# Two-part products with 512 moving columns for the memory keys, MoBA and cross-attention queries

## Chip, cores and metric

The program runs on one core of a Trainium2 chip (trn2). The metric is device time of one execution in microseconds (us), the median of several runs. The engines are TensorE (PE; its weight loads are shown apart as PEld), VectorE (DVE), ScalarE (ACT), GpSimd (POOL) and SyncE (SP), each with a queue that it works off in order.

## What is computed

A decoder trunk of two layers on 256 tokens of width 1024. Each layer is a SwiGLU half-step, a mixing step (RWKV-7 on 8 heads beside causal attention, called MoBA, on 8 heads), cross-attention to 256 memory tokens, and a second SwiGLU half-step:

```python
x = x + 0.5 * swiglu_ffn(rms_norm(x, ffn1_norm_g[l]), ffn1_w_in[l], ffn1_w_out[l])
proj = rms_norm(x, mix_norm_g[l]) @ w_mix_in[l]        # RWKV columns, then q_m, k_m, v_m of MoBA
x = x + concat([rwkv7_time_mix(...), moba_attention(q_m, k_m, v_m, rel_bias)]) @ w_mix_out[l]
x = x + memory_cross_attention(rms_norm(x, ..), rms_norm(mem, ..), w_q[l], w_kv[l], w_o[l])
x = x + 0.5 * swiglu_ffn(rms_norm(x, ffn2_norm_g[l]), ffn2_w_in[l], ffn2_w_out[l])
```

All is float32. The products that concern us are `q_m` and `k_m` (512 columns each), the memory keys (1024 columns of `w_kv`) and the cross-attention queries `h @ w_q` (1024 columns).

## The kernel before

**Two parts.** An operand of a large product is split into a high part that TensorE takes exactly (`fp32r`) and the low rest: `split` (L85) makes the high part with a copy on ACT and the rest with a subtraction on DVE. A product is the sum of high times high, high times low and low times high. `mm3` (L96) issues these as three matmuls into one sum.

**Weights.** `load` (L101) brings a unit of 1 MB into one of two `raw` buffers with a transfer on SP; `unit` splits it into two halves `whi`, `wlo` (five buffers each; two ACT copies, two DVE subtractions of 1024 columns). A half is one column tile: 128 output columns of all 1024 rows, which are 8 K-tiles. A `raw` buffer is free for the next transfer once its second DVE subtraction is done.

**Feature-major products.** The operand is `xt`, laid out `[k // 2][:, k % 2, high or low, token]`, so that high and low tokens of one K-tile lie side by side (512 columns). `col_a` (L250) makes one column tile, `[128, 256]`, with 8 times `mm3`: 24 matmuls of 256 moving columns. `proj_a` (L256) puts the two column tiles of a unit side by side in one PSUM bank. The `ffn` (L308) already uses another form (L329 to L338): high weights times both parts in one matmul of 512 columns, low weights times the high part in one of 256, then an ACT copy of the second half of the bank to `z` and a DVE addition of the first half to it.

**The mixing step** (`mix`, L849). `rwkv` (L531) is written as a generator; between its steps TensorE is given other work: `early` (MoBA queries and keys, four units), then, after the operand of the memory tokens is made (`mem_operand`, L368: eight ACT copies, eight DVE operations of 256 columns), `others`: MoBA's heads, `late` (memory keys, four units), values of the memory tokens, and the first output products. `early` and `late` both call `pieces` (L880): two column tiles by `col_a` into one bank, then one ACT copy of 512 columns to `dst`. The generators yield a number of microseconds that steers how much filling is put between two steps. In RWKV's stretch of masked chunk products each chunk and half takes four matmuls on PE and two DVE products (`XB`, `ZL`, L653 and L655); an inverse by rows follows on DVE (`pr`, `mb`, L691).

**Cross-attention** (`xattn`, L378). `scores(h)` makes a head's queries with `proj_a`, splits them from PSUM (one ACT copy, one DVE subtraction of 512 columns, `put_pair`), multiplies them with the keys, and takes the softmax; `mixv(h - 1)` follows with the values of the head before.

**Buffers and order.** Four PSUM banks carry the tag `acc`; `z` has tag `k1` with six buffers, which RWKV's `ub`, `mb`, `pr`, `T1`, `TB`, `R` share. The order on each queue is made by the framework's planner from priorities, dependencies and its own costs; it may place instructions of different lines between each other.

Of the kernel before, what the change touches and what calls it, by code (L numbers as in the profile page):

```python
# [12 lines left out]
OP = mybir.AluOpType  # L13
# [3 lines left out]
S = 256  # L17
L = 2
DFF = 2816
NB = DFF // 256  # L20
KT = D // 128
# [26 lines left out]
def body(tc, ctx, I, out):  # L48
# [52 lines left out]
    def load(src, cuts, heap=False):  # L101
        """A unit of weights: its two halves' exact high and low parts, and the pieces that make them."""
        raw = wp.tile([128, 2048], FT, name=nm("raw"), tag="raw", bufs=2)
        loads.append(nc.sync.dma_start(raw, src).ins)
        halves, pieces = [], []
        for i in range(2):
            if heap:
                hi, lo = (H([128, 1024], FR, "wb") for _ in range(2))
            else:
                hi, lo = (wp.tile([128, 1024], FR, name=nm(t), tag=t, bufs=WB) for t in ("whi", "wlo"))  # L110
            w = 1024 // cuts
            for c in range(0, 1024, w):
                pieces.append((hi[:, c:c + w], lo[:, c:c + w], raw[:, i * 1024 + c:i * 1024 + c + w]))
            halves.append((hi, lo))
        return halves, pieces
# [11 lines left out]
    def rsqrt(v, n, tag):  # L127
        """1 / (RS sqrt(v)): the exponent's half as a first guess, a third-order step and a Newton
        step, each step's factor left in."""
        r = SM([128, n], name="rs", tag=tag)  # L130
        t = SM([128, n], name="rt", tag=tag)
        V.tensor_scalar(r.bitcast(I32), v.bitcast(I32), -0.5, float(0x5F3759DF), op0=OP.mult, op1=OP.add)

        def square():
            if n == 1:
                stt(t, r, v, r, OP.mult, OP.mult)
            else:
                tt(t, r, r, OP.mult)
                tt(t, t, v, OP.mult)

        square()
        stt(t, t, -10.0 / 3.0, t, OP.add, OP.mult)
        stt(r, t, 5.0, r, OP.add, OP.mult)
        square()
        stt(r, t, -3.0 * (8.0 / 3.0) ** 2, r, OP.add, OP.mult)
        return r

# [43 lines left out]
    def XT(tag="xn"):  # L191
        """Operand with 1024 rows on partitions: [k // 2][:, k % 2, high or low, token]."""
        return [H([128, 2, 2, S], FR, "xt", tag) for _ in range(4)]
# [10 lines left out]
    def normed(g):  # L204
        """Norm of x with gain g into a new operand, a tile of 128 tokens at a time."""
        xT = []

        def do(t, pieces=()):
            """Between its feature tiles, pieces of weights are split."""
# [21 lines left out]
    def proj_b(xT, ws):  # L231
        """Token-major [2][128, 512]; all of the first 128 tokens, then the others."""
        ws = [tuple(a.rearrange("p (k n) -> p k n", k=2) for a in h) for h in ws]
        acc = []
        for t in range(2):
            acc.append(BANK("acc"))
            for k in range(KT):
                mm3(acc[t], tok(xT, k, t), tuple(a[:, k % 2, :] for a in ws[k // 2]),
                    k == 0, k == KT - 1)
            yield acc[t]  # L240
# [3 lines left out]
    def ahead(src, u):  # L244
        """A unit of the next stage's first block, split ahead."""
        if u == 0:
            ready.clear()
        ready.extend(unit(src[u], CU["b"], True))

    def col_a(acc, xT, w):  # L250
        """Feature-major [128, 256] of one column tile."""
# [3 lines left out]

    def proj_a(xT, src, cuts):  # L256
        """Feature-major [128, 2, 256] of one unit of two column tiles."""
# [5 lines left out]
    def proj_out(lhs, src, nk, scale, post, following=None, split_tail=False):  # L263
        """x += scale * lhs @ w, token-major over 1024 columns; units of two K-tiles. post(t)
        follows each tile of tokens. following: the weights of the next stage's first block."""
# [42 lines left out]
    def ffn(xT, w_in, w_out, post, following, early=()):  # L308
# [17 lines left out]
        for j in range(2, DFF // 128):  # L326
            sums = []
            for half_ in unit(w_in[j], CU["ffn"]):
                w = tuple(a.rearrange("p (k m) -> p k m", k=KT) for a in half_)  # L329
                acc = BANK("acc")  # L330
                for k in range(KT):
                    mm(acc, w[0][:, k, :], xT[k // 2][:, k % 2].rearrange("p i t -> p (i t)"),
                       k == 0, False)
                    mm(acc[:, 0:S], w[1][:, k, :], feat(xT, k)[0], False, k == KT - 1)
                z = SM([128, S], name="z", tag="k1")
                copy(z, acc[:, S:2 * S])
                tt(z, acc[:, 0:S], z, OP.add)
                sums.append(z)  # L338
# [39 lines left out]
    def xattn(l, xT, kTf, vx, post, following):  # L378
        """vx: the values of the memory tokens by pairs of heads, and what makes the second pair."""
# [8 lines left out]
        def scores(h):  # L388
            put_pair(qT, h, proj_a(xT, I["w_q"][l, h], CU["q"]))
# [63 lines left out]
    def moba(qT, kT, v, yT):  # L453
        """Steps of one head each: its scores, then the values of the head before."""
# [76 lines left out]
    def rwkv(l, xT, yT):  # L531
        """Yields the time, in us of TensorE, that its next step waits for."""
# [10 lines left out]
        def shifted(u, dst):  # L543
            """One unit of two column tiles: p + (shift(p) - p) * mu, tokens along the free axis."""
# [33 lines left out]
        # decay products inside a chunk  # L578
# [9 lines left out]
        # normalised keys, negated  # L588
# [16 lines left out]
        # k * (1 + (a - 1) * k_a)  # L605
# [17 lines left out]
        # operands of the chunk products  # L623
# [17 lines left out]
        # products inside a chunk: transposed, masked  # L641
# [26 lines left out]
        # inverse of I - U: 16x16 diagonal blocks, one to a partition  # L668
# [8 lines left out]
        # token-major b/G, k/G  # L677
# [87 lines left out]
        # bonus and gate: y * (g * ln_g) + (r k r_k v + ln_b) * g  # L765
# [7 lines left out]
        # chunks in order  # L773
        for c in range(NCH):
# [48 lines left out]
            # group norm over each head, two chunks at once  # L823
# [25 lines left out]
    def mix(l, xT, post):  # L849
# [8 lines left out]
        def v_block(mT, n):  # L858
            """Values of the memory tokens, heads 2n and 2n + 1: [token tile][128, high or low, 512]."""
# [20 lines left out]
        def pieces(xT, src, dst):  # L880
            """Two column tiles into dst [128, 2, 256], one at a time."""
            acc = BANK("acc").rearrange("p (c t) -> p c t", c=2)
            for c, w in enumerate(unit(src, CU["qk"])):
                col_a(acc[:, c, :], xT, w)
                if c:
                    copy(dst, acc)
# [102 lines left out]
def _onehot(np):  # L989
    """Column m: the bucket of distance 255 - m."""  # L990
# [7 lines left out]
def _layout(np, z):  # L998
    z = {k: np.asarray(v) for k, v in z.items()}

    def k_rows(w, kt, n):
        """(L, K, N) into units of kt K-tiles: (L, K/(128 kt), 128, kt*N)."""
# [4 lines left out]
    def col_pairs(w):  # L1007
        """(L, 1024, N) into units of two column tiles: (L, N/256, 128, 2*8*128)."""
# [4 lines left out]
    def blocks(w):  # L1013
        """(L, 1024, N) into blocks of 512 columns, two units each: (L, N/256, 128, 4*512)."""
# [4 lines left out]
    def gate_up(w):  # L1019
        """The first 256 gate and 256 up columns as a block, then a gate and an up column tile a unit."""  # L1020
# [62 lines left out]
```

## Time and profile before

| | us |
|---|---|
| median of 3 runs | 1321.84 (1321.48 to 1321.96) |
| span of the profiled execution, first to last instruction | 1317.5 |
| PE busy in it | 1294.7 |
| DVE busy | 913.3 |
| ACT busy | 769.3 |
| HBM read | 217.70 MB, 168 GB/s over the span |

The runs' times hold some 4.3 us that lie outside the span; another time of the profiled execution is not given. Busy times of engines overlap. The granted TensorE clock was 0.998 of its full speed over the span. Matmuls overlap in the records (a matmul of 256 columns is shown with 0.28 us and the next one begins 0.12 us after it), so the pace of TensorE is read from starts, not from durations.

### The profile page before, as it was taken

What the parts mean: (1) busy time and instruction counts of PE and PEld (TensorE: products, weight loads), DVE (VectorE), ACT (ScalarE), POOL (GpSimd) and SP (SyncE); (2) the same over time, 40 slices, a digit from 0 to 9 for tenths busy, and PEclk for the clock granted to TensorE, in tenths of its full rate; (3) what the DMA queues carried; (4) which work ended last, traced back from release to release, by engine and by line L of the source; (5) the groups of instructions that cost most, each with busy time, mean ns of one, the idle gap of its engine ahead of it and who ended that gap; (6) DMA issues with size and microseconds to landing.
All of it is one profiled execution on the core that took longest, in us unless ns stands there. A gap on an engine that the chain in (4) does not pass through costs nothing.

```text
span 1317.5 us, 21984 instructions
## 1 busy us (share of the span) xinstructions
PE 1294.7 (98%) x8722; PEld 1109.7 (84%) x8722; DVE 913.3 (69%) x1699; ACT 769.3 (58%) x1465; POOL 33.7 (3%) x49
## 2 busy tenths in 40 slices
PE   7999999999999999999999999999999999999997
PEld 5888888998878988888888888889887798888886
DVE  6766656698588676665577775558976976776644
ACT  6755546749656555555455554475685565655533
POOL 0000000020000000000000000000200000000000
PEclk9999999999999999999999999999999999999999
DMA  6775563334234445555735556433341354355552
GB/s 213 263 278 193 192 255 113 130 127 140 87 134 166 149 151 174 187 193 192 250 105 191 190 192 223 177 128 128 129 146 66 128 193 157 147 187 189 185 179 92
DMA packets 32919, 221.22 MB, mean 168 GB/s; under 512 B 4248, under 2 KB 4384, under 8 KB 7344
## 3 DMA queue, kind: packets, MB, share of 16 engines
q1 hardware_dynamic: 30064, 210.54, 45.0%
q0 software_dynamic: 2176, 8.44, 1.9%
q8 instruction: 68, 1.11, 0.3%
q10 hardware_dynamic: 576, 0.85, 0.2%
q14 instruction: 35, 0.29, 0.1%
HBM read 217.70 MB, written 3.68 MB: 168 GB/s over the span
## 4 chain that ended last, share of the span: by engine, by line
PE 85%; DVE 8%; ACT 4%; DMA 2%; issue 1%; ACTq 0%
PE acc L94 77%; PE pm L94 5%; DVE wlo L77 2%; DVE ZL L77 1%; PE tr L188 1%; DVE XB L77 1%; ACT whi L83 1%; DMA raw<-in_w_k_dram 1%; ACT xt L83 1%; ACT junk L174 0%; DVE wb L77 0%; PE acc L500 0%; DMA raw<-in_w_q_dram 0%; DVE rt L80 0%; ACT e L400 0%
## 5 line engine op out<-in xcount | busy, mean ns | idle before, releaser
L94 PE MATMUL acc<-xt,whi 128*128 128x512 f32 (+1 forms) x2496 | 681.6, 344 | 1.0 <-DVE xt L80 0.7
L77 DVE TENSOR_TENSOR wlo<-raw,whi 128x1024 fp32r<-128x1024 f32 (+1 forms) x456 | 465.1, 1034 | 257.9 <-ACT whi L83 256.5
L83 ACT ACTIVATE whi<-raw 128x1024 fp32r<-128x1024 f32 (+1 forms) x456 | 405.3, 906 | 331.8 <-PE acc L94 240.7
L94 PE MATMUL acc<-xt,wlo 128*128 128x256 f32 x1888 | 529.8, 281 | 0.2 <-DVE wlo L77 0.2
L94 PEld LDWEIGHTS acc<-xt,whi 128*128 128x128 f32 x2496 | 431.7, 189 | 64.5 <-issue 2.8
L94 PEld LDWEIGHTS acc<-xt,wlo 128*128 128x128 f32 x1888 | 357.3, 189 | 3.0 <-issue 1.4
L94 PE MATMUL acc<-whi,hT 128*128 128x512 f32 x704 | 220.9, 393 | 0.0
L94 PEld LDWEIGHTS acc<-whi,hT 128*128 128x128 f32 x704 | 132.3, 188 | 29.9
L94 PE MATMUL acc<-wlo,hT 128*128 128x512 f32 x352 | 138.2, 393 | 0.0
L94 PEld LDWEIGHTS acc<-wlo,hT 128*128 128x128 f32 x352 | 66.2, 188 | 14.7
L77 DVE TENSOR_TENSOR z<-acc,z 128x256 f32<-128x256 f32 x160 | 66.7, 417 | 0.3 <-ACT z L83 0.2
L83 ACT ACTIVATE xt<-tr,par 128x128 fp32r<-128x128 f32 x128 | 43.9, 364 | 32.9 <-PE tr L188 18.4
L94 PE MATMUL acc<-wb,xt 128*128 128x512 f32 x240 | 61.4, 399 | 0.0
L83 ACT ACTIVATE z<-acc 128x256 f32<-128x256 f32 x160 | 58.6, 366 | 1.8 <-PE acc L94 1.7
L94 PE MATMUL acc<-whi,xt 128*128 128x512 f32 x160 | 57.2, 420 | 1.2 <-ACT xt L83 1.1
L94 PEld LDWEIGHTS acc<-wb,xt 128*128 128x128 f32 x240 | 43.4, 188 | 9.4 <-ACT xt L83 0.4
L80 DVE SCALAR_TENSOR_TENSOR xt<-tr,par,xt 128x128 fp32r<-128x128 f32 x128 | 41.4, 345 | 11.2 <-ACT xt L83 11.0
L174 ACT ACTIVATE junk<-x 128x512 f32<-128x512 f32 x36 | 22.7, 632 | 33.9 <-DVE x L80 25.1
L94 PE MATMUL acc<-whi,oT 128*128 128x512 f32 x128 | 40.3, 393 | 0.0
L77 DVE TENSOR_TENSOR z<-z,z 128x256 f32<-128x256 f32 x80 | 34.0, 425 | 8.4 <-DVE z L77 0.9
L83 ACT ACTIVATE hT<-z 128x256 fp32r<-128x256 f32 x80 | 32.2, 403 | 10.3 <-DVE z L77 10.1
L94 PEld LDWEIGHTS acc<-whi,xt 128*128 128x128 f32 x160 | 31.2, 198 | 8.2 <-ACT xt L83 1.4
(224 smaller groups left out, 1226.2 us busy)
## 6 DMA issues: line engine op xcount, KB each, us to landing
raw<-in_w_f1i_dram SPq DMA_DIRECT2D x44, 1024.0 KB, 4.8
raw<-in_w_f2i_dram SPq DMA_DIRECT2D x44, 1024.0 KB, 4.7
raw<-in_w_f1o_dram SPq DMA_DIRECT2D x22, 1024.0 KB, 4.8
raw<-in_w_mixa_dram SPq DMA_DIRECT2D x22, 1024.0 KB, 4.7
raw<-in_w_f2o_dram SPq DMA_DIRECT2D x22, 1024.0 KB, 4.8
raw<-in_w_k_dram SPq DMA_DIRECT2D x8, 1024.0 KB, 4.8
raw<-in_w_v_dram SPq DMA_DIRECT2D x8, 1024.0 KB, 4.8
raw<-in_w_mixo_dram SPq DMA_DIRECT2D x8, 1024.0 KB, 4.7
```

Source lines behind the costliest of these rows:

```text
L77: V.tensor_tensor(out=out_, in0=a, in1=b, op=op)
L80: V.scalar_tensor_tensor(out_, a, s, b, op0=op0, op1=op1)
L83: return A.activation(out_, in_, AF.Copy, **k)
L94: nc.tensor.matmul(o, a, b, start=start, stop=stop, skip_group_check=True)
L174: marks["square"] = A.activation(junk, xt[:, n * 512:(n + 1) * 512], AF.Square, scale=1.0 / 32.0, accum_out=ss[:, n:n + 1]).ins
L188: nc.tensor.transpose(p[:, k, :], xs[:, k * 128:(k + 1) * 128], ident)
```

## The change

`col_sum` is a new function, taken from the body of `ffn`, which now calls it; what `ffn` issues stays the same. `pieces` and `scores` call it in place of `col_a` and `proj_a`. `proj_a` with `col_a` remain for RWKV's own columns. Comments and docstrings fall away too.

```diff
+    def col_sum(dst, xT, w):
+        w = tuple(a.rearrange("p (k m) -> p k m", k=KT) for a in w)
+        acc = BANK("acc")
+        for k in range(KT):
+            mm(acc, w[0][:, k, :], xT[k // 2][:, k % 2].rearrange("p i t -> p (i t)"), k == 0, False)
+            mm(acc[:, 0:S], w[1][:, k, :], feat(xT, k)[0], False, k == KT - 1)
+        z = SM([128, S], name="z", tag="k1")
+        copy(z, acc[:, S:2 * S])
+        if dst is None:
+            dst = z
+        tt(dst, acc[:, 0:S], z, OP.add)
+        return dst
...
         def scores(h):
-            put_pair(qT, h, proj_a(xT, I["w_q"][l, h], CU["q"]))
+            for c, w in enumerate(unit(I["w_q"][l, h], CU["q"])):
+                split(qT[h][:, c, 0, :], qT[h][:, c, 1, :], col_sum(None, xT, w))
...
         def pieces(xT, src, dst):
-            acc = BANK("acc").rearrange("p (c t) -> p c t", c=2)
             for c, w in enumerate(unit(src, CU["qk"])):
-                col_a(acc[:, c, :], xT, w)
-                if c:
-                    copy(dst, acc)
+                col_sum(dst[:, c, :], xT, w)
                 yield 2.6
```

Over both layers it touches 16 column tiles each of `early`, `late` and `scores`: 48 tiles of 8 K-tiles.

## Rows read from the trace of the kernel before

**Rows 1.** The page: the span, busy time by engine, and the chain that ended last by engine.

```profile
span 1317.5 us, 21984 instructions
PE 1294.7 (98%) x8722; PEld 1109.7 (84%) x8722; DVE 913.3 (69%) x1699; ACT 769.3 (58%) x1465; POOL 33.7 (3%) x49
PE 85%; DVE 8%; ACT 4%; DMA 2%; issue 1%; ACTq 0%
```

**Rows 2.** Busy time by stretch; columns: stretch, its length, then PE, PEld, DVE, ACT and POOL busy (instructions), granted clock, DMA share, GB/s. In order: RWKV's masked chunk products with `early`, in both layers; the rest of RWKV with `others`, in both layers; cross-attention, in both layers.

```profile
268.00:300.00 32.00, 32.00 (x266) 30.68 (x266) 30.54 (x53) 17.23 (x26) 7.89 (x8) 1.00 0.38 132
914.00:946.00 32.00, 32.00 (x266) 30.54 (x264) 29.07 (x50) 17.22 (x27) 7.89 (x8) 1.00 0.34 114
300.00:382.00 82.00, 80.90 (x1133) 65.38 (x1132) 58.87 (x143) 58.76 (x139) 3.52 (x6) 1.00 0.32 111
946.00:1028.00 82.00, 80.07 (x1130) 65.10 (x1128) 59.64 (x144) 58.27 (x137) 1.50 (x2) 1.00 0.30 105
412.00:462.00 50.00, 49.40 (x358) 45.61 (x357) 34.50 (x67) 29.52 (x64) 0.00 (x0) 1.00 0.42 148
1062.00:1108.00 46.00, 45.62 (x339) 42.34 (x338) 31.39 (x60) 26.21 (x55) 0.55 (x1) 1.00 0.44 158
```

**Rows 3.** Timeline of PE in `early`, layer 0: the low-weight matmul of a K-step and the one 26 K-steps later, without other work between them.

```profile
287.67 0.28 PE L94 MATMUL acc<-xt,wlo 128*128 128x256 f32 x1
...
297.03 0.28 PE L94 MATMUL acc<-xt,wlo 128*128 128x256 f32 x1
```

**Rows 4.** Timeline of PE in `ffn`: the low-weight matmul of a K-step and a later one; 28 K-steps apart in layer 0, 11 K-steps apart in layer 1.

```profile
59.81 0.28 PE L94 MATMUL acc<-xt,wlo 128*128 128x256 f32 x1
...
69.70 0.28 PE L94 MATMUL acc<-xt,wlo 128*128 128x256 f32 x1
...
690.91 0.27 PE L94 MATMUL acc<-xt,wlo 128*128 128x256 f32 x1
...
694.72 0.28 PE L94 MATMUL acc<-xt,wlo 128*128 128x256 f32 x1
```

**Rows 5.** Tiles named `z`: durations in ns (min/median/max); the copy and the addition of `ffn`'s form, and the two operations of a split of 256 columns.

```profile
L83 ACT ACTIVATE z<-acc x160: 362/365/385, 32.9 to 1250.1; 128x256 f32<-128x256 f32 x160
L77 DVE TENSOR_TENSOR z<-acc,z x160: 413/417/426, 34.3 to 1251.4; 128x256 f32<-128x256 f32 x160
L83 ACT ACTIVATE hT<-z x80: 397/401/420, 37.6 to 1252.4; 128x256 fp32r<-128x256 f32 x80
L77 DVE TENSOR_TENSOR hT<-z,hT x80: 349/418/427, 38.9 to 1252.8; 128x256 fp32r<-128x256 f32 x80
```

**Rows 6.** Timeline of ACT, 262 to 300 us: the copies of `early` at the ends of its first three units, and the memory operand behind a weight split.

```profile
275.49 0.60 ACT L83 ACTIVATE mqk<-acc 128x512 f32<-128x512 f32 x1 [3.70 <-PE acc L94]
...
285.44 0.60 ACT L83 ACTIVATE mqk<-acc 128x512 f32<-128x512 f32 x1 [4.41 <-PE acc L94]
...
293.70 0.58 ACT L83 ACTIVATE mqk<-acc 128x512 f32<-128x512 f32 x1
296.64 1.06 ACT L83 ACTIVATE whi<-raw 128x1024 fp32r<-128x1024 f32 x1 [2.36 <-DMA raw<-in_w_k_dram]
297.60 1.69 ACT L83 ACTIVATE xt<-memT,par 128x256 fp32r<-128x256 f32 x4
```

**Rows 7.** Chain of waits, 262 to 312 us and 908 to 958 us (start, length, what): the last links on DVE before the transfer, and the transfer.

```profile
288.78 0.69 DVE ZL L77
289.48 2.28 DVE wlo L77 x2
291.77 4.79 DMA raw<-in_w_k_dram
...
935.25 2.28 DVE wlo L77 x2
937.54 4.80 DMA raw<-in_w_k_dram
```

**Rows 8.** Timeline of DVE, 262 to 345 us: the one idle time over 0.1 us between 262 and 299 us, the low parts of the memory operand, and a step of the inverse behind them.

```profile
269.29 0.48 DVE L80 SCALAR_TENSOR_TENSOR rkv<-acc,par,rkv 128x255 f32<-128x255 f32 x1 [0.53 <-ACT rkv L83]
...
299.42 3.25 DVE L80 SCALAR_TENSOR_TENSOR xt<-memT,par,xt 128x256 fp32r<-128x256 f32 x8
...
303.76 0.21 DVE L77 TENSOR_TENSOR pr<-mb,ub 128x64 f32<-128x64 f32 x1
```

**Rows 9.** Timeline of PE around 300 us (layer 0: the first matmuls on the memory operand, and a wait), and PE's waits from 914 to 958 us (layer 1: us in total, times, longest).

```profile
300.41 0.50 PE L94 MATMUL acc<-xt,whi 128*128 128x256 f32 x2
...
302.48 0.66 PE L682 MATMUL tr<-con,BK 128*128 128x128 f32 x4 [0.25 <-ACT BT L83]
...
PE acc L94 <- DVE xt L80: 0.7, 1, 0.7
PE acc L500 <- ACT lg L83: 0.7, 1, 0.7
```

**Rows 10.** Timeline of all engines in cross-attention, layer 0, from the end of the last head's queries on.

```profile
449.99 0.60 ACT L83 ACTIVATE xt<-acc 128x512 fp32r<-128x512 f32 x1 [0.90 <-PE acc L94]
...
450.62 0.69 DVE L77 TENSOR_TENSOR xt<-acc,xt 128x512 fp32r<-128x512 f32 x1 [0.81 <-ACT xt L83]
...
457.15 0.39 PE L94 MATMUL acc<-whi,oT 128*128 128x512 f32 x1
...
457.62 0.60 PE L412 MATMUL tr<-con,e 128*128 128x128 f32 x4
```

More of the change, by code (lines that the diff above doesn't have):

```diff
@@ L328, in ffn @@
             for half_ in unit(w_in[j], CU["ffn"]):
[L329 to L338, printed above, removed]
+                sums.append(col_sum(None, xT, half_))
             A.activation(sums[0], sums[0], AF.Silu)
```

## The prediction

> **What bounds the kernel now.** I read the page first: PE is busy 1294.7 of 1317.5 us and holds 85% of the chain that ended last [rows 1]. So a saving of TensorE time counts, if nothing else is late in the same stretch. The second view is busy time by stretch, for the three places that the change touches [rows 2]. In `early`'s stretch PE is busy all 32.0 us, but DVE is busy 30.5 (layer 0) and 29.1 (layer 1): two engines are full there. After it PE is idle for 1.1 and 1.9 us of 82, and in cross-attention for 0.6 and 0.4 us; DVE is at 72 and 69% there in layer 0. The third view is the chain of waits over `early`'s stretch [rows 7]: although PE never idles, the chain runs down DVE, masked products and weight splits in turn, to the transfer of a `w_k` unit at 291.77. The reader is to see there that the end of this stretch hangs on DVE: the split frees a `raw` buffer, the transfer lands 4.8 us later, ACT stands 2.4 us waiting for it, and only behind that come its copies of the memory operand [rows 6], on which the next filling work of PE depends.
>
> **PE's saving.** Columns streamed stay the same: 3 x 256 before, 512 + 256 after. What falls away is one matmul and one weight load in three. Before, 26 K-steps of `early` take 297.03 - 287.67 = 9.36 us, 0.360 us each [rows 3]. `ffn` has the new form already: 28 K-steps in 69.70 - 59.81 = 9.89 us, 0.3532 us each, in layer 0; 11 in 3.81 us, 0.3464 each, in layer 1 [rows 4]. The saving is 6.8 ns a K-step in layer 0 and 13.6 in layer 1, taking each layer's own pace; I know no reason for the difference, so both ends stay in the range for all steps. Each of the three places has 8 tiles x 8 = 64 K-steps a layer: 0.44 us in layer 0, 0.87 in layer 1, 1.3 for each place over both layers, 3.9 for all three (bounds 384 x 6.8 ns = 2.6 and 384 x 13.6 ns = 5.2).
>
> Here a rule speaks against the change. The trace shows a 256-column matmul 0.12 us after the one before [rows 3]. The Trainium skill, TensorE: Matmul & The Clock Gate, section Back-to-back issue gap, gives a warm gap of N/2.4 + 2.5 ns for N columns: a removed matmul would save only its fixed 2.5 ns, by estimate 384 x 2.5 ns = 1.0 us in place of 3.9. The trace's K-steps are longer than that rule on both sides and differ by more, so I go by the rows.
>
> **What is added.** Each of 48 tiles gets an ACT copy of 0.365 us and a DVE addition of 0.417 us [rows 5]. `pieces` loses one ACT copy of 0.60 us a unit [rows 6]: ACT +0.13 us, DVE +0.83 us a unit, 16 units. `scores` keeps its split, now two of 0.401 and 0.418 us from SBUF in place of one of 0.60 and 0.69 us from PSUM [rows 5, 10]: ACT +0.93 us and DVE +0.98 us a unit, 8 units. In all some 21 us more DVE work and 10 us more ACT work. ACT has room in `early`'s stretch (17 of 32 us busy), so its part goes at nothing there; DVE has none.
>
> **Early: the addition on DVE's chain.** The first two units of `early` end at 275.5 and 285.4, the third at 293.7 [rows 6]. So four tiles are done by 285.4 and a fifth about half way to 293.7: five additions become due before the two splits that free the buffer at 291.77, and layer 1 repeats it before 937.54 [rows 7]. Eight DVE operations of 256 columns in a row take 3.25 us, 0.41 each [rows 8], so five are 2.05 us; the only free time in this run is 0.53 us [rows 8]. I take 1.5 us of delay for the transfer, for the split that ACT waits for, and for the memory operand queued on ACT behind it. The bounds are 0 (the planner moves these two splits ahead of masked products, which is open to it) and 8 x 0.417 = 3.3 us (all additions end up ahead of the low parts at 299.4). What PE loses: in layer 1 it already waits on the low part of the operand, 0.7 us [rows 9], so all 1.5 us. In layer 0 the low part of the first K-tile is done at about 299.42 + 0.41 = 299.8 and PE begins on it at 300.41 [rows 8, 9]: some 0.5 us are covered, 1.0 us is lost. Together +2.5 us. And because DVE sets the end of this stretch, `early`'s own 1.3 us of PE time buy nothing.
>
> **Late.** PE is the bound again, with 1.3 us of gain. The additions fall where DVE is at 72% and the keys are not needed before the cross-attention, so I cost them at nothing, covered by MoBA's and RWKV's matmuls; if a waiting addition holds RWKV's serial steps behind it in DVE's queue (the inverse's `pr` and `mb`, behind the operand at 303.76 [rows 8]), up to 0.365 us a time is lost, 16 x 0.365 = 5.8 us at the most, below nothing not at all.
>
> **Cross-attention.** Gain 1.3 us. For heads 0 to 2 the values of the head before and the next queries cover the longer way out. For head 3 it was 0.60 + 0.69 = 1.29 us after the last matmul [rows 10] and becomes 0.365 + 0.417 + 0.401 + 0.418 = 1.60: 0.3 us later. PE's filling ends with the matmul at 457.15 and the transposes behind the softmax come at 457.62 [rows 10]: no cover is left, so 0.3 us a layer, 0.6 in all (bounds 0, since the first of the two tiles is now ready earlier, and 0.6 a layer, if the weight splits that stand on DVE there come between).
>
> **Buffers, at nothing.** A tile now takes a bank of its own, but holds it 2.9 us of matmuls and about 0.8 us more; four banks cover that while MoBA holds two. `z` finds three of six `k1` buffers free even while `ub`, `mb`, `pr` live. If that fails, PE waits for one addition, 0.4 us a time.
>
> **The sum**: -1.3 (late) - 1.3 (cross-attention) + 2.5 (early) + 0.6 (last head) = +0.5 us on the profiled span of 1317.5, so 1318.0. The runs lie 4.3 us above the span before; that stays. Forecast 1322.3 us, no change that can be told: a difference of 0.2% (2.6 us) is about the least that a measurement of this kernel shows.
>
> **Rivals.** (a) The additions are hidden in `early`. The planner orders DVE with them in view; the two splits can go ahead of masked products whose result PE doesn't need at once, since PE has filling work to the end of the stretch. For it: PE idles nowhere in 268 to 300. Against it: the chain there is on DVE with 0.03 us gaps, and DVE's work has to be done before the inverse anyway. It gives all 3.9 us less the 0 to 0.6 us of the last head: 1317.9 to 1318.5, say 1318.1. Chance 0.27.
>
> (b) Slower: DVE's queue decides. All eight additions of `early` stand before the operand's low parts, 3.3 us in each layer, PE waits for all of it, 6.6 us, with 0.6 for the last head and 2.6 of gain in the other two places: +4.6, 1326.4 us. It decides as soon as the delay at the end of `early` is over some 2.3 us a layer. For it: DVE at 95% in layer 0. Against it: three of the eight tiles end after the transfer has been asked for, when DVE in layer 1 has room. Chance 0.23.
>
> (c) The change doesn't do what it says: a K-step stays at 0.360 us in these stretches, because what is streamed sets the pace and not the number of matmuls. Then no 2.6 us, +3.1, 1324.9 us. Against it are the `ffn` rows with the same weights and operand layout. Chance 0.05; with the skill's fixed gap (section above) it would be about 256 x 2.5 ns = 0.6 us better than this, by estimate.
>
> **How the numbers follow.** Forecast (gain eaten, 1320 to 1324.4 with its bounds): 0.45. With (a) faster 0.27, the forecast same 0.45, (b) and (c) slower 0.28. The range reaches down to (a) with some of its bound, 1317.3, and up to (b), 1326.8; what is left out is a pace of 0.3464 everywhere with nothing lost, and `late`'s blocked steps on top of (b).
>
> **What would show it.** K-steps of 0.346 to 0.353 us in `early`, `late` and the queries show the saving; 0.360 shows (c). 384 fewer matmuls, 48 more DVE additions, 16 fewer copies of 512 columns. In `early`'s stretch the `w_k` transfer should start some 1.5 us later against the end of RWKV's columns, and PE should idle before the first matmul on the memory operand; no later transfer shows (a), over 2.3 us shows (b). PE idle of more than 2 us over `late` would be the blocked steps. A time under 1319.2 or over 1324.4 makes the prediction wrong.

## The result and the profile after

The changed kernel takes 1338.34 us (median of 4 runs, 1337.02 to 1339.66) against 1321.66 of the kernel before on the same chip: 1.0129 times as long, 95% interval 1.0117 to 1.0141, 16.7 us slower. The forecast was 1322.3, with a range to 1326.8. The profiled execution has a span of 1335.2 us, 17.7 more than before [rows 1]. That execution as a whole took 1337.02 us, so 1.8 us lie outside its span, as in the later runs of the kernel before. Of the 4.3 us between the span before and its median, the other 2.5 are then an execution that was faster than the median. One run each of `own_bank_two` (1414.6 us) and `late_five` (1833.7, the profiled one) had a much lower granted clock, 0.85 and 0.65, and is left out of the figures below.

The page of the changed kernel: span, busy time by engine, and the chain by engine.

```profile
span 1335.2 us, 21325 instructions
PE 1300.7 (97%) x8338; PEld 1091.5 (82%) x8338; DVE 928.0 (69%) x1755; ACT 776.6 (58%) x1505; POOL 31.5 (2%) x49
PE 91%; DVE 4%; ACT 3%; DMA 1%; issue 1%; ACTq 0%
```

The counts are as predicted: 384 matmuls fewer; 56 DVE operations more, which are 48 additions and 8 splits; 40 ACT copies more. DVE is busy 14.7 us longer and ACT 7.3, less than the 21 and 10 that were added up. Yet PE is busy 6.0 us longer, although it has less to do. The place shows in the busy time by stretch. Columns as in [rows 2]; the second fence has the same stretch of layer 0 in the kernel before.

```profile
268.00:300.00 32.00, 31.90 (x202) 26.93 (x201) 29.96 (x46) 17.93 (x34) 6.76 (x8) 1.00 0.36 120
300.00:345.00 45.00, 38.61 (x569) 29.35 (x567) 32.60 (x94) 31.55 (x78) 1.48 (x2) 0.85 0.26 92
946.00:1028.00 82.00, 74.66 (x910) 58.32 (x909) 55.85 (x142) 55.63 (x134) 3.22 (x4) 0.92 0.30 102
423.00:473.00 50.00, 49.87 (x304) 43.48 (x304) 40.42 (x84) 34.33 (x78) 0.00 (x0) 1.00 0.45 161
```

```profile
300.00:345.00 45.00, 43.90 (x709) 37.09 (x708) 32.54 (x85) 39.47 (x100) 1.48 (x2) 1.00 0.32 107
```

In `early`'s stretch (268 to 300) and in cross-attention (423 to 473 here, since it begins 10.9 us later than before) PE is about as busy as it was. Behind 300, in the rest of RWKV with MoBA and `late`, two things are new: PE idles 6.4 us of 45 in place of 1.1, and the granted clock is 0.85 in place of 1.00. In the clock record, two stretches of 6.83 us in each layer stand at 0.50, the lower level, from 307.0, 330.9, 962.4 and 986.3. The kernel before has none in its mixing steps. The whole mixing step of layer 0, before and after, from its first copy of `mv` to its last output product:

```profile
213.31:403.69 190.38, 188.80 (x1903) 164.89 (x1902) 147.49 (x314) 125.32 (x255) 11.88 (x14) 1.00 0.37 129
212.38:414.57 202.19, 194.25 (x1775) 160.93 (x1774) 152.29 (x330) 126.52 (x263) 10.76 (x14) 0.97 0.34 121
```

PE idles 7.9 us in place of 1.6, 6.4 more; 13.66 us at half clock cost up to 6.8; 128 shorter K-steps give back 1.8 (14 ns each, see below). That makes 11.4, and the step is 11.8 us longer.

Marks on the way through the mixing step, from the starts in the two timelines, in us from its first copy of `mv` (213.31 before, 212.38 after in layer 0; 859.11 and 868.14 in layer 1), layer 0 / layer 1. `M` holds the inverse's finished blocks, `W` is built from them, and the product of `W` and `R` comes with the first chunk of the recursion:

| | before | after |
|---|---|---|
| last masked chunk product (PE) | 73.5 / 73.4 | 75.4 / 75.4 |
| first `ub` of the inverse (DVE) | 79.1 / 79.1 | 87.0 / 87.0 |
| last `pr` of the inverse (DVE) | 99.2 / 99.9 | 110.4 / 110.2 |
| first product of `W` and `R` (PE) | 135.7 / 136.5 | 146.3 / 146.0 |
| last output product (PE) | 190.4 / 191.1 | 202.2 / 201.9 |
| last product on `oT`, cross-attention (PE) | 265.4 / 266.0 | 275.3 / 274.6 |

So the inverse starts 8 us late and ends 10 to 11 late; the mixing step loses 11.8 and 10.8; cross-attention then takes 75.0 / 74.9 us before and 73.1 / 72.7 after, a gain of about 2 us a layer.

What stands ahead of the inverse: timeline of DVE, after, layer 0.

```profile
295.16 0.41 DVE L77 TENSOR_TENSOR mqk<-acc,z 128x256 f32<-128x256 f32 x1
295.49 1.21 DVE L77 TENSOR_TENSOR wlo<-raw,whi 128x1024 fp32r<-128x1024 f32 x1
296.65 0.42 DVE L77 TENSOR_TENSOR mqk<-acc,z 128x256 f32<-128x256 f32 x1
297.41 2.08 DVE L80 SCALAR_TENSOR_TENSOR xt<-memT,par,xt 128x256 fp32r<-128x256 f32 x5 [0.34 <-ACT xt L83]
299.41 0.43 DVE L681 TENSOR_SCALAR ub<-UT,con 128x256 f32<-128x256 f32 x1
...
323.27 0.38 DVE L700 TENSOR_REDUCE mb<-pr 128x15 f32<-128x225 f32 x1
```

The same two operations before:

```profile
292.40 0.46 DVE L674 TENSOR_SCALAR ub<-UT,con 128x256 f32<-128x256 f32 x1
...
313.17 0.38 DVE L693 TENSOR_REDUCE mb<-pr 128x15 f32<-128x225 f32 x1
```

Before, `ub` ran at 292.40 and the operand's low parts came seven us behind it [rows 8]. After, additions, weight splits and five of the eight low parts come first. Counted from the step's start, the low parts come 1.1 us earlier than before (2.7 in layer 1), and PE begins on the memory operand at 87.8 us in both layers, against 87.1 and 88.2.

The weight transfer that the prediction watched did move. It begins at 293.57, 81.2 us after the step's start, against 78.5 before [rows 7], 2.7 us later in both layers. But ACT no longer waits for it ahead of the operand: the eight copies now stand in front of that unit's split. The transfer, and ACT's timeline, after, layer 0:

```profile
293.57 0.33 SPq L104 DMA_DIRECT2D raw<-in_w_k_dram  x1
```

```profile
296.87 2.51 ACT L83 ACTIVATE xt<-memT,par 128x256 fp32r<-128x256 f32 x6 [0.25 <-PE acc L94]
...
299.54 0.90 ACT L83 ACTIVATE xt<-memT,par 128x256 fp32r<-128x256 f32 x2
...
302.58 1.05 ACT L83 ACTIVATE whi<-raw 128x1024 fp32r<-128x1024 f32 x1
```

What PE does then: timeline of PE, after, layer 0, with K-steps of `early`, the two waits, and the first K-steps behind them.

```profile
296.90 0.27 PE L94 MATMUL acc<-xt,wlo 128*128 128x256 f32 x1
...
298.63 0.28 PE L94 MATMUL acc<-xt,wlo 128*128 128x256 f32 x1
...
300.23 0.50 PE L94 MATMUL acc<-xt,whi 128*128 128x512 f32 x1
...
304.53 0.66 PE L722 MATMUL tr<-con,rkv 128*128 128x128 f32 x4
307.18 1.09 PE L507 MATMUL acc<-con,lg 128*128 128x128 f32 x3 [1.99 <-ACT lg L83]
309.31 1.54 PE L94 MATMUL acc<-mpT,mv 128*64 128x128 f32 x6 [1.04 <-ACT mpT L83]
...
311.38 0.42 PE L94 MATMUL acc<-xt,wlo 128*128 128x256 f32 x1
...
312.02 0.41 PE L94 MATMUL acc<-xt,wlo 128*128 128x256 f32 x1
```

Five K-steps of `early` take 298.63 - 296.90 = 1.73 us, 0.346 each: the change does what it says. Then PE waits 1.99 us for the softmax of MoBA's first head (`lg`) and 1.04 for the copy of its transposes (`mpT`), and the next K-steps take 0.64 us. Before, the same wait was filled with the second column tile of the unit:

```profile
306.05 0.66 PE L715 MATMUL tr<-con,rkv 128*128 128x128 f32 x4
306.46 0.48 PE L94 MATMUL acc<-xt,whi 128*128 128x256 f32 x2
...
308.17 0.33 PE L500 MATMUL acc<-con,lg 128*128 128x128 f32 x1 [0.27 <-ACT lg L83]
```

The second half-clock stretch of layer 0 lies by a wait for the late inverse. The chain of waits, after, from 324 on, runs down DVE, RWKV's operations and weight splits in turn, to `W` (start, length, what), and PE's timeline has the wait for it:

```profile
324.68 1.13 DVE wlo L77
325.81 0.97 DVE M L707
...
327.25 1.12 DVE wlo L77
328.37 0.97 DVE W L707
```

```profile
329.48 0.63 PE L94 MATMUL tr<-T,W 32*32 32x32 f32 x29 [1.14 <-DVE W L707]
```

### The profile page after: what moved, and what is told of

It reads as the page before. It is cut to its first block, busy times and chain, and to the rows that moved or that the text cites. A ratio compares the mean times of both kernels' runs of the same rounds, so it can differ in the third digit from the quotient of the medians.

```text
span 1335.2 us, 21325 instructions
## 1 busy us (share of the span) xinstructions
PE 1300.7 (97%) x8338; PEld 1091.5 (82%) x8338; DVE 928.0 (69%) x1755; ACT 776.6 (58%) x1505; POOL 31.5 (2%) x49
## 4 chain that ended last, share of the span: by engine, by line
PE 91%; DVE 4%; ACT 3%; DMA 1%; issue 1%; ACTq 0%
PE acc L94 82%; PE pm L94 6%; PE tr L188 1%; DVE wlo L77 1%; DMA raw<-in_w_f1i_dram 1%; ACT whi L83 1%; ACT junk L174 1%; DVE rt L80 0%; PE tr L94 0%; PE acc L507 0%; PE tr L689 0%; PE tr L848 0%; DVE xs L184 0%; DVE M L77 0%; ACT lg L494 0%
## 5 line engine op out<-in xcount | busy, mean ns | idle before, releaser
L94 PEld LDWEIGHTS acc<-xt,whi 128*128 128x128 f32 x2112 | 383.9, 189 | 77.6 <-issue 3.8
L83 ACT ACTIVATE z<-acc 128x256 f32<-128x256 f32 x208 | 76.3, 369 | 21.4 <-PE acc L94 21.2
L94 PEld LDWEIGHTS acc<-wlo,hT 128*128 128x128 f32 x352 | 66.2, 188 | 14.7
L77 DVE TENSOR_TENSOR z<-acc,z 128x256 f32<-128x256 f32 x176 | 73.3, 417 | 0.5 <-ACT z L83 0.3
L83 ACT ACTIVATE hT<-z 128x256 fp32r<-128x256 f32 x80 | 32.2, 403 | 10.9 <-DVE z L77 10.9
```

Source lines behind the costliest of these rows:

```text
L77: V.tensor_tensor(out=out_, in0=a, in1=b, op=op)
L83: return A.activation(out_, in_, AF.Copy, **k)
L94: nc.tensor.matmul(o, a, b, start=start, stop=stop, skip_group_check=True)
```

## The experiments

The theories, as they stood before the runs. **A**: in `late` it is the column tile's own bank that costs; the unit's second tile no longer fills PE beside a MoBA head. Later it was parted into **A1** (the tile lacks a free bank) and **A2** (the planner orders it behind the head). **B**: in `early` the additions on DVE put the inverse late. **C**: once PE has idled, the halved clock costs as much again. **D** and **E** are the rivals of C and A2: the half clock isn't from the idle time; the additions and the longer hold of a bank cost most by themselves. Ratios are to runs of the kernel before on the same chip, with their 95% interval; "half clock" is the time at 0.50 in both layers' mixing steps, of the profiled execution.

| kernel | us | ratio | half clock, us |
|---|---|---|---|
| after | 1338.3 | 1.0129 (1.0117 to 1.0141) | 27.3 |
| q_only | 1318.6 | 0.9977 (0.9965 to 0.9989) | 0 |
| early_only | 1336.6 | 1.0115 (1.0096 to 1.0133) | 17.1 |
| early_inverse_first | 1325.3 | 1.0028 (1.0017 to 1.0039) | 3.4 |
| early_pool | 1325.7 | 1.0039 (1.0025 to 1.0053) | 3.4 |
| late_only | 1344.3 | 1.0167 (1.0152 to 1.0182) | 23.9 |
| own_bank | 1328.9 | 1.0051 (1.0034 to 1.0068) | 13.7 |
| own_bank_two | 1328.4 | 1.0062 (1.0038 to 1.0087) | 10.2 |
| own_bank_filled | 1338.1 | 1.0126 (1.0109 to 1.0143) | 17.1 |
| before_five | 1357.3 | 1.0274 (1.0256 to 1.0292) | 0 (13.7 behind them) |
| late_five | 1387.2 | 1.0491 (1.0473 to 1.0508) | not known |
| before_between | 1330.5 | 1.0076 (1.0061 to 1.0091) | 6.8 |
| late_between | 1327.6 | 1.0049 (1.0034 to 1.0064) | 0 |
| before_pairs | 1340.3 | 1.0132 (1.0097 to 1.0168) | 17.1 |
| late_pairs | 1332.7 | 1.0092 (1.0072 to 1.0112) | 6.8 |
| late_pool | 1336.8 | 1.0124 (1.0097 to 1.0151) | 20.5 |
| queries_early_mended | 1316.5 | 0.9957 (0.9941 to 0.9974) | 0 |
| all_mended | 1335.9 | 1.0109 (1.0093 to 1.0125) | 23.9 |
| all_pairs | 1337.2 | 1.0138 (1.0084 to 1.0192) | 20.5 |

**One place at a time.** In each of three kernels only one of the three callers has the new form; the others keep the old `pieces` or `proj_a`.

```diff
-                    yield from pieces(xT, I["w_mixa"][l, 7 + 2 * i + j], z[j])
+                    yield from pieces_old(xT, I["w_mixa"][l, 7 + 2 * i + j], z[j])
```

> Only the cross-attention queries in the new form, MoBA's and the memory keys' products as before. In the changed kernel the stretch from the first output products of the mixing step to the end of cross-attention became 1.8 and 2.1 us shorter (layers 0 and 1). Theory B (the additions of `early` and `late` on DVE push RWKV's inverse back) and theory A (PSUM banks: a tile of `late` holds an `acc` bank of its own until its addition has run, and MoBA's heads wait for banks) agree here: 1317.5 to 1319.5 us, 2.2 to 4.2 faster than before. If the queries' part costs too (rival C), it is 1321 or more.

> Only `early` (MoBA's queries and keys) in the new form. Theory B: the eight additions a layer delay the inverse; half or more of the loss of some 11 us a layer stays, 1330 us or more, with PE idle and a clock under 1.00 between 300 and 345 us. Theory A: `early` shares its banks with nobody else, so 1320 to 1324 us and a clock of 1.00 there.

> Only `late` (memory keys) in the new form. Theory A: the loss is here, 1332 to 1342 us, with PE idle before MoBA's transposes around 305 us. Theory B: the additions of `late` come after the weights for them are split, so 1320 to 1326 us.

The queries alone gain 3 us. `early` alone loses 15 and `late` alone 22, so neither theory was enough: A had `early` at no loss, and B `late`. Together with the queries' gain the loss is only 16.7, so the two don't add. The marks show that they sit in different stretches: with `early` alone the first product with `M` is 11.8 / 11.1 us late, and the way from there to the product of `W` and `R` is shorter than before (26.5 / 28.8 us against 32.5 / 32.6); with `late` alone it is 3.3 / 4.3 us late, and that way takes 39.9 us; in the changed kernel it is 11.3 / 10.5 us late, and the way takes 31.8.

**The bank alone.** The old three matmuls of 256 columns, no addition, but for each tile in `early` and `late` a bank and an ACT copy of its own.

```diff
-            acc = BANK("acc").rearrange("p (c t) -> p c t", c=2)
             for c, w in enumerate(unit(src, CU["qk"])):
-                col_a(acc[:, c, :], xT, w)
-                if c:
-                    copy(dst, acc)
+                acc = BANK("acc")
+                col_a(acc[:, 0:S], xT, w)
+                copy(dst[:, c, :], acc[:, 0:S])
```

> `early` and `late` with the matmuls of before (3 x 256 columns a K-step) and no addition, but each column tile in an `acc` bank of its own, copied out by one ACT copy of 256 columns; the queries as before. It takes the bank apart from the addition and from the 512 columns. Theory A: most of the loss is here too, 1330 us or more. Theory B: no addition on DVE, so 1320 to 1324 us.

It costs 7 us, under the 1330 that A expected and not most of the loss. Up to the end of the inverse its marks are within 0.8 us of those of the kernel before; behind it, the first product of `W` and `R` is 5.5 / 4.7 us late. Its timeline of PE has the two waits of the changed kernel:

```profile
306.89 0.84 PE L506 MATMUL acc<-con,lg 128*128 128x128 f32 x3 [1.61 <-ACT lg L83]
309.29 1.54 PE L94 MATMUL acc<-mpT,mv 128*64 128x128 f32 x6 [1.56 <-ACT mpT L83]
```

So neither additions nor 512 columns are needed for the stall: there A holds. The rest of `late_only`'s loss, some 15 us, isn't explained by it. The marks show where most of it arises: on the way from the first product with `M` to that of `W` and `R`, 39.9 us a layer against 34.6 in `own_bank` and 32.5 before. On that way ACT stands idle for 9.6 us in front of weight splits that wait for PE (0.9 in `own_bank`, 0.3 before), with RWKV's copies behind them in its queue. Timeline of ACT, `late_only`, layer 0:

```profile
336.53 1.06 ACT L83 ACTIVATE whi<-raw 128x1024 fp32r<-128x1024 f32 x1 [4.73 <-PE acc L94]
...
337.89 0.38 ACT L83 ACTIVATE T<-pm 128x256 f32<-128x256 f32 x1
```

Whether these splits are the cause is not shown.

**Why the second tile stands back.** Two ways of giving it its bank: a fifth bank with the tag `acc` (taken from `tr`), beside a control that has the fifth bank alone; and both banks of a unit asked for when the unit begins.

```diff
-BANKS = {"acc": 4, "tr": 2, "pm": 2}
+BANKS = {"acc": 5, "tr": 1, "pm": 2}
```

> Control for the next run: the kernel before with five PSUM banks of tag acc and one of tag tr in place of four and two. Nothing of the change is in it. Both theories leave it free; by estimate it loses a few us where two transposes no longer overlap with the copy of the one before, 1322 to 1330.

> Only the memory keys in the new form (as in the run that gave 1344.3 with four banks), with five banks of tag acc and one of tag tr. Theory A1 (a shortage: the second tile of a unit finds no free bank): with a fifth bank the tile is free to run, TensorE no longer idles behind the first MoBA head, no stretch at a granted clock of 0.50, and the time comes to within 3 us of the control with five banks. Theory A2 (no shortage but an order: once the tile is a group of its own, the planner puts its matmuls behind the transposes and values of the MoBA head, which wait for softmax): the idle time of about 3 us a layer and the half clock stay, 12 us or more above the control.

```diff
+            banks = [BANK("acc") for _ in range(2)] if both else None
             for c, w in enumerate(unit(src, CU["qk"])):
-                acc = BANK("acc")
+                acc = banks[c] if banks else BANK("acc")
```

> The run with a bank of its own for each tile (1328.9), but for the memory keys both banks of a unit are asked for when the unit begins, as the one bank was before. Theory A1 (the second tile waits for a bank to be handed out behind the MoBA head's): it has its bank now, so the 3.2 us of idle time and the half clock go and the time returns to 1321 to 1324. Theory A2 (the planner's order): TensorE works off the MoBA head first all the same, idle time and half clock stay, 1326 to 1331.

With five banks the new form of `late` costs 30 us over its control (1387.2 against 1357.3; the control itself lost far more than expected). With the banks asked for early the time is that of `own_bank`, and PE waits as it does there:

```profile
307.57 0.83 PE L506 MATMUL acc<-con,lg 128*128 128x128 f32 x3 [1.63 <-ACT lg L83]
```

A1 falls: a free bank doesn't bring the filler back. What remains, by elimination, is the order that the planner makes once the tile is a group of its own.

**Another order.** If A2 holds, the new form should cost nothing in an order of the text in which the tile stands ahead of the head's values. Two such orders, each with a control in which only the order is changed: a tile between a head's scores and the values of the head before; and both tiles of a unit between two heads.

```diff
             if h < 8:
                 scores(h)
+            yield 0.8
             if h:
                 values(h - 1)
-            yield 1.6
+            yield 0.8
...
-            for w in att:
+            for n, w in enumerate(att):
                 yield w
-                yield from islice(ks, 1)
+                if n % 2 == 0:
+                    yield from islice(ks, 1)
```

> Control: the kernel before with that same new order of MoBA's steps and nothing else. Both theories: 1318 to 1326 us, so that late_between can be read against it.

> As late_only (1344 us), but each tile of `late` is asked for between a MoBA head's scores and the values of the head before, in place of behind both, so that a second tile has its bank before the transposes do and stands ahead of them on PE. Theory A (the wait at 305 us is PE standing at the transposes because the next tile of `late` got no `acc` bank): the 3 us of PE idle and the half clock behind it go, 1318 to 1328 us. If the additions of `late` on DVE are the cause, the order of the filling changes little: 1338 to 1346 us.

```diff
-                yield from islice(ks, 1)
+                yield from islice(ks, 2)
```

> Control: the kernel before with both column tiles of a unit of memory keys asked for between two MoBA heads, in place of one tile between two heads. Nothing of the change is in it. Softmax of a head then has 5.8 us of matmuls beside it, but the keys are used up after four heads. By estimate 1318 to 1330; both theories leave it free.

> Only the memory keys in the new form (DVE additions, a bank for each tile), both tiles of a unit between two MoBA heads. Theory A2 (what costs is that the second tile stands behind a head whose softmax isn't done): both tiles now stand ahead of it, so no wait of over 1 us for the head's weights, no stretch at a granted clock of 0.50 at 305 to 315, and the time is within 4 us of the control. Theory E (the additions and the longer hold cost most by themselves): 8 us or more above the control.

In both orders the new form isn't slower than its control: the medians are 2.9 us (1327.6 against 1330.5) and 7.5 us (1332.7 against 1340.3) lower, with intervals that just overlap, where in the order of the kernel before it was 22.2 slower. That speaks for A2 and against E, though the controls lose time of their own in these orders and could hide a cost. The wait for `lg` is gone from 305 to 315 in both, and in the first so is the half clock. The windows of 305 to 310 and 310 to 315, first `late_only`, then `late_between`:

```profile
305.00:310.00 5.00, 2.67 (x13) 1.41 (x11) 4.18 (x17) 4.90 (x17) 0.77 (x1) 0.81 0.15 35
310.00:315.00 5.00, 4.50 (x15) 3.79 (x16) 4.79 (x10) 4.96 (x9) 0.00 (x0) 0.51 0.29 68
```

```profile
305.00:310.00 5.00, 3.80 (x22) 2.85 (x20) 4.17 (x16) 4.93 (x15) 0.77 (x1) 1.00 0.12 20
310.00:315.00 5.00, 4.55 (x26) 3.67 (x27) 4.93 (x15) 4.18 (x8) 0.00 (x0) 1.00 0.68 244
```

Three expectations missed: the orders themselves cost 9 us (1318 to 1326 was expected) and 17 to 20 us, and in `late_pairs` the wait for `mpT` stayed (2.04 us), with a half-clock stretch of 3.4 us behind it.

**The clock.** `own_bank` with filler in the idle time: ahead of the first head's transposes, six matmuls of constants into the bank that the transposes then overwrite, in each layer (the trace lists each as two).

```diff
+            if h == 0:
+                for _ in range(6):
+                    mm(q[:, 0:2, :].rearrange("p k t -> p (k t)"), ident, con[:, 0:S])
             for k in range(3):
                 nc.tensor.transpose(q[:, k, :], lg[:, k * 128:(k + 1) * 128], ident)
```

> The run with a bank of its own for each tile (three matmuls of 256 columns, no additions) plus idle filler: ahead of the first MoBA head's transposes, six 128x256 matmuls of constants into the bank that the transposes then overwrite, in each layer; nothing else is computed with them. In the unfilled run TensorE idled 3.2 us there (1.6 and 1.6), then ran 6.83 us at a granted clock of 0.50 in each layer, and the profiled span was 1327.7. Theory C (the idle time costs twice, once itself and once through the clock behind it): the 0.50 stretches at 308.8 and 960.7 are gone or shorter, K-steps behind the mpT product are 0.36 us again in place of 0.64, the idle time itself stays lost to filler work, and the span falls by 4 to 7 us, to 1321 to 1324. Theory D (the half clock comes from what stands in the stretch and not from the idle time, or its time is covered by other waits): 0.50 stretches stay or the span stays at 1326 to 1329.

At the place itself C holds. Timeline of PE of the filled kernel:

```profile
304.86 2.86 PE L94 MATMUL acc<-con 128*128 128x256 f32 x12
307.56 0.49 PE L509 MATMUL acc<-con,lg 128*128 128x128 f32 x3
...
309.72 0.87 PE L94 MATMUL acc<-mpT,mv 128*64 128x128 f32 x6 [1.23 <-ACT mpT L83]
...
310.86 0.28 PE L94 MATMUL acc<-xt,wlo 128*128 128x256 f32 x1
...
311.21 0.28 PE L94 MATMUL acc<-xt,wlo 128*128 128x256 f32 x1
```

The granted clock stays at 1.00, a K-step takes 0.36 us in place of 0.64, and the first product with `M` comes 104.15 us after the start of the step, against 106.63 without filler and 103.24 in the kernel before. But the time as a whole got worse by 9 us, and the span of 1336.1 is what neither C nor D expected. The filler shifts the planner's order again, and, as in `late_only`, at 321 a weight split that had to wait for PE stands on ACT ahead of the softmax and of copies that RWKV needs:

```profile
321.06 1.06 ACT L83 ACTIVATE whi<-raw 128x1024 fp32r<-128x1024 f32 x1 [1.99 <-PE acc L94]
...
323.10 0.38 ACT L83 ACTIVATE TB<-tr 32x256 f32<-32x256 f32 x1
```

From 324 to 327 PE is busy 1.36 us of 3, and 6.83 us at 0.50 begin at 324.4. So the link from idle time to half clock is shown at one place; its share of the whole isn't.

**Early: whose turn on DVE.** In the first kernel the inverse's first steps stand in the text ahead of the memory operand; in the second the two halves are copied out by ACT and added on GpSimd. Both have the new form in `early` alone.

```diff
-        yield None
 
         UT = SM([128, 16, 2, 16], name="UT", tag="k2")
...
         V.tensor_copy(mb, con[:, C_EYE:C_EYE + 256].rearrange("p (a b) -> p a b", a=16))
+        yield None
```

```diff
-                col_sum(dst[:, c, :], xT, w)
...
+                copy(z, acc[:, S:2 * S])
+                copy(dst[:, c, :], acc[:, 0:S])
+                nc.gpsimd.tensor_tensor(out=dst[:, c, :], in0=dst[:, c, :], in1=z, op=OP.add)
```

> As early_only (1337 us), but the first steps of RWKV's inverse (the transpose, `ub`, `mb`) stand ahead of the rest of `early` and of the memory operand in the kernel's text. Theory B (the additions fill DVE, so that the operand's low parts, which come earlier in the text, take DVE first and `ub` starts 8 us later): `ub` returns to about 79 us after the mixing step's start and the time to 1320 to 1327 us. If the late masked products (2 us) are what counts, the time stays at 1332 or more.

> As early_only, but the sum of a tile's halves is made on GpSimd, after two ACT copies; DVE gets no addition. Theory B: masked products end at 73.5 and `ub` starts at 79 us again, 1317 to 1323 us. If the loss comes from the 512-column matmuls or from banks, it stays at 1330 or more.

Each brings back some 11 of the 15 us. In the first, DVE's timeline has the inverse ahead of the low parts again:

```profile
294.38 0.44 DVE L679 TENSOR_SCALAR ub<-UT,con 128x256 f32<-128x256 f32 x1
...
298.45 2.05 DVE L80 SCALAR_TENSOR_TENSOR xt<-memT,par,xt 128x256 fp32r<-128x256 f32 x5
```

`ub` starts 81.7 / 83.6 us after the start of the step, not at the expected 79, and the inverse ends at 105.8 / 106.8 in place of 110.0 / 110.0. In the second `ub` stays late (86.2 / 88.1), although DVE has no addition there and even idles ahead of the low parts:

```profile
296.63 2.16 DVE L80 SCALAR_TENSOR_TENSOR xt<-memT,par,xt 128x256 fp32r<-128x256 f32 x5 [1.48 <-ACT xt L83]
298.71 0.43 DVE L680 TENSOR_SCALAR ub<-UT,con 128x256 f32<-128x256 f32 x1
```

Yet the inverse takes 16.5 us in place of 22.9 and ends at 102.7 / 104.6; the time missed the expectation by 3 us. So B holds for the end of the inverse, and not for its start: where `ub` stands is the planner's order, and that changed without an addition on DVE too. Nor does each us of lateness cost one: with the first product with `M` 8.3 / 8.7 us late, `early_inverse_first` has mixing steps only 1.9 / 0.9 us longer than before; with 11.8 / 11.1 us late, `early_only` has them 5.6 / 7.3 us longer, 17.1 us at half clock included. The new order of the text was not run without the change, so a part of what it brings may be its own.

**GpSimd for `late`, and versions of the whole.** `late_pool` is `late_only` with GpSimd's sums. `queries_early_mended` has the queries and `early` new, with both of `early`'s mends, and `late` old. `all_mended` and `all_pairs` add `late` in the new form: the first with GpSimd's sums and a tile between scores and values, the second with DVE's sums and two tiles between heads.

> As late_only (1344 us; own_bank, without sums, 1329 us), but the sum of a tile's halves is made on GpSimd after two ACT copies, so that the `acc` bank is free when the second copy is done. If the hold of the bank up to the DVE addition makes the 15 us between those two, it comes to own_bank: 1325 to 1332 us. If the 512-column matmuls themselves make it, it stays at 1338 or more.

> The queries in the new form (3 us gained alone), `early` in the new form with its sums on GpSimd and the inverse's first steps ahead in the text, the memory keys as before. Theory B: with no addition on DVE and the inverse in its place, `early` costs nothing and may give 0 to 1.3 us: 1317 to 1320 us. If something else of the new form costs in `early`, 1321 to 1325.

> All three places in the new form, sums of `early` and `late` on GpSimd, the inverse's first steps ahead, a tile of `late` asked for between scores and values. Theories A and B: both causes are met, no half clock inside the mixing step; the order of the filling cost 9 us alone (before_between) and 6 with late_only, so 1318 to 1328 us, 10 or more below the changed kernel (1338). If neither is the cause, 1333 or more.

> Queries new, MoBA queries and keys new with the sums on GpSimd and the inverse's first steps ahead of the memory operand (together 1316.5), and memory keys new with DVE sums, both tiles of a unit between two MoBA heads. A2 and a control that costs nothing: 1314 to 1318. Theory E: 1324 or more.

`late_pool` brings back about a third of `late`'s loss, half of what lay between `late_only` and `own_bank` and between the two expectations: it tells nothing apart. `queries_early_mended` is faster than both kernels, 5 us below the kernel before (0.9957). But no gain of `early` is shown: the interval overlaps that of `q_only`, and in its profiled execution (the slowest of the four, 1319.7 us) the mixing steps take 192.1 / 192.0 us against 190.4 / 191.1 before, while cross-attention takes 72.8 in both layers against 75.0 / 74.9.

The two that add `late` lose 20 us on it and missed their expectations; the orders which suit `late` cost 9 us and 17 to 20 us by themselves in their controls, which leaves some 10 us of the first without a cause. No version was found in which `late` in the new form pays.

## Why the prediction was wrong

- **PE's saving** was right in kind and nearly in size: 0.346 us a K-step, the lower of the two paces, 14 ns saved. Rival (c) falls. By the formula in the Trainium skill, TensorE: Matmul & The Clock Gate, section Back-to-back issue gap, only 2.5 ns a K-step would have been saved; the section gives it for an isolated matmul and says that in a stream of weight loads and matmuls both set the spacing. The 14 ns measured decide against using it for this stream.
- **Cross-attention** gained more than the 1.3 us less 0.6 of the sum: 1.9 and 2.1 us a layer, and 3 us in the run with the queries alone. The last head's 0.6 us never came: PE is busy 49.87 of the 50 us from 423 to 473, and the last head's transposes, at 466.19, follow a matmul without a wait. Of the gain 64 x 14 ns = 0.9 us a layer is the K-steps, and 0.5 / 0.2 us is idle time that is gone; the rest wasn't traced.
- **Early: the addition on DVE's chain** had the delay and got its path to PE wrong. The transfer came 2.7 us later in each layer, more than the 1.5 us of the sum and over the 2.3 that were to show rival (b). What failed is the step that only behind the transfer and its split come ACT's copies of the operand: the planner put the copies ahead of that split, PE didn't wait for the operand at all, and the term of +2.5 us never came. What came last on DVE instead is RWKV's inverse: it starts 8 us late behind splits and low parts, and `early` alone costs 15 us. The prediction had the inverse in view, but as work "behind the operand" that could be blocked in `late` for 5.8 us at the most; it was late already in `early`. Rival (b), DVE's queue, is nearest in kind; its sign came, its price, 6.6 us on PE's wait for the operand, did not.
- **"Buffers, at nothing"** failed. Nothing shows that four banks were too few: a fifth one and banks asked for early brought nothing (`late_five`, `own_bank_two`). What it missed is what the shared bank did: it let the second tile run beside a head's softmax. The tile as a group of its own is put behind the head, and PE waits not "0.4 us a time" but 3.0 us in a row (1.99 and 1.04). `own_bank` prices that at 7 us, without additions and without 512 columns. Why the planner orders it so stays open; of the other 15 us of `late_only` only the place is known, behind the inverse, where ACT stands in front of weight splits.
- **The clock** stood in no term of the sum. The kernel before holds 1.00 through its mixing steps; the changed one spends 27.3 us at 0.50, worth up to 13.7 us of the 22.6 that the two mixing steps lose. In layer 0 that is up to 6.8 us beside 6.4 us of added idle time, so here a price worked out from waits alone would have been too small by up to a factor of two. By the table the kernels without half clock lie between -5 and +6 us of the kernel before, `before_five` apart, and those with 17 us or more of it at +14 to +22. The table alone doesn't say which comes first; the filled run does, for one place. The Trainium skill, TensorE: Matmul & The Clock Gate, section A second HAM failure mode: psum-queue depth-cycling, tells of a kernel in which cycling through banks left PE idle so often that the clock swung between the two levels. This trace agrees as far as the swing goes (four stretches at 0.50 in the two mixing steps); what left PE idle here was the softmax and the late inverse.

## What to carry to other kernels

Before a product gets a bank of its own, ask what the shared one let the scheduler do: two tiles in one group were the filler that covered another engine's softmax. An operation added to an engine that is 95% busy need not delay its own consumer: here the scheduler put a serial chain last, so look for that chain in the queue. A new order of the text needs a control that has the order alone: two such controls lost 9 us and 17 to 20 us. Where TensorE holds its full clock through a stretch, price a stall of a few us there at its length and up to as much again, and look at the granted clock of the stretch behind it.

## What was not expected of the hardware

In the changed kernel the granted clock fell to 0.50 at 307.0, within a wait of 1.99 us, and stayed there for 6.83 us, although PE idled only 1.2 us of that; in `own_bank_filled`, with the first wait filled and 1.23 us of the second left, it stayed at 1.00 there. Waits spread thinner, as in `late_between` (PE busy 3.80 of 5 us, then 4.55 of 5), left it at 1.00 too.
